# A planned transformer step on one Trainium2 core: ranges kept by column, a rotation's four swaps issued together, and the attention sink as one more column of the scores

## The chip, the cores and the metric

The kernel runs on one core of one Trainium2 chip. The metric is the device time of one execution in microseconds (us). A core has five engines that run side by side: TensorE (PE in the profile, its weight loads PEld), VectorE (DVE), ScalarE (ACT), GpSimd (POOL) and SyncE (SP), which here issues nearly all DMAs. Every engine works through its own list of instructions in order and waits on semaphores for the others.

## The reference

Two layers of a backbone work on 128 context tokens and 512 latent tokens at once (640 columns), with 2048 features. Each layer norms and modulates its input (adaLN), projects it, runs two mixers, gates the result and projects it out. The modulation is a product of a conditioning vector with a large matrix. The change lies in mixer A of layer 0, the windowed attention of eight query heads over two key/value heads, with rotated queries and keys and a sink logit per head:

```python
out = jnp.stack([a * cos - b * sin, a * sin + b * cos], axis=-2)      # rope_2d, for each axis
...
sk = jnp.broadcast_to(sink.astype(jnp.float32).reshape(1, 1, KV_A, g, 1, 1), s_ctx.shape[:-1] + (1,))
p = jax.nn.softmax(jnp.concatenate([s_band, s_ctx, sk], axis=-1), axis=-1)
pb = p[..., :3 * BAND_BLK]
pc = p[..., 3 * BAND_BLK:3 * BAND_BLK + L]
```

The sink takes part in the softmax's maximum and sum, and its own probability is dropped.

## The kernel before

**The work.** Activations lie feature-major: 128 features on the partitions, 640 tokens in the columns. A projection is cut into chunks of 128 output features. A chunk is 16 input tiles, times two halves of the columns, times three products of split float32 operands (`whi`/`wlo` with `acth`/`actl`, line 400): 96 matmuls of 320 or 322 columns. The chunks of the two layers are most of what TensorE does. In the later parts seven products stand for eight block products. While a chunk runs, the other engines split the next weights (ACT makes `whi`, POOL makes `wlo`), take the last chunk out of PSUM, and do the mixers' elementwise work. A slow background task makes the modulation: it loads a row block of the adaLN matrix, 256 KB (`adas<-ada`, `adas<-ada_g`), and reduces it on DVE (`CUSTOM_DVE_ANT_0 adas<-adas,bank`) or by POOL and ACT (`prod`).

**The order.** No scheduler of the compiler decides the order. The program is written out by `Trunk`, which keeps a clock of its own (`self.now`, TensorE's) and a cost model, `Pace`. `Pace.record` (reached from `Engine.call`, line 215, so nearly every VectorE, ScalarE and GpSimd row of the profile has that line) adds each instruction's reckoned time to its engine. `Pace.note` marks which columns of which tile are written and read until when, and `Pace.ready` says from when an operand can be used. The marks go by the ranges of `Pace.span`. Mixers are Python generators: `tick`, called every two matmuls of a chunk, resumes those whose reckoned waits are over (`until`, `bank`), and what they issue lands between the chunk's matmuls at that place. So a wrong reckoning costs no correctness, since semaphores guard all data, but it puts an instruction too early, and its engine then stands still with all that is queued behind it.

`Trunk.dma` (line 436) issues a DMA on SP at once if the model holds both ends ready within 0.1 us; otherwise it puts it into `pc.late`, and it is issued when it is reckoned ready or when another instruction touches its range.

**`span`.** `ap.offset` of an on-chip view counts in elements with the partition's stride in it. A view that starts at partition 32 of a tile 512 columns wide so gets a range that begins 32 rows further on, where no other view of that tile has marks.

**`rope`** (line 1606) rotates one head's 512 latent columns. Pairs of 32-partition strips of `q` are exchanged into `sw` by four DMAs of 64 KB, then DVE multiplies `q` by `cos`, POOL multiplies `sw` by `sin`, and DVE adds them. It is called ten times: for two keys and eight queries. `sw` is a strip of `arena` or of `Y`, so in the profile the swaps read `arena<-Y`, `Y<-arena` and `arena<-arena`. Three of the four swaps have a source that begins at partition 32 or more; the one that reads partition 0 has a range that the model has marked as being written.

**`even_head`** takes a head's five query blocks (one of context, four latent) through `blocks`: `s1` makes the scores and calls `soft1`, `soft2` scales, `s3` transposes the probabilities by TensorE (line 405, `bank<-ident,arena`) and ACT copies them out; one pass at the end multiplies with the values. `soft1` adds the mask and takes the row maximum (DVE), forms `nm` = -max(maximum, sink), and runs Exp with the row sum in `den` (ACT). Then ACT forms `es` = Exp(sink + nm). `soft2` adds `es` to `den` on ACT, takes the reciprocal on DVE and scales on ACT. Layer 1's attention calls the same two functions without a sink. `open_att` lays out the attention's part of SBUF; `pieces` are the four score buffers of 512 columns.

Of the kernel before, what the change touches and what calls it, by code (L numbers as in the profile page):

```python
# [13 lines left out]
AF = mybir.ActivationFunctionType  # L14
# [38 lines left out]
class Pace:  # L53
# [19 lines left out]
    def span(self, ap):  # L73

        if ap.space == bass.MemoryType.DRAM and ap.name not in (SPILL, YSP, SHIFTS, *KEEP):
            return None
        name = self.slot.get(ap.name, ap.name)
        if ap.space == PSUM:
            return name, 0, 1
        lo = hi = ap.offset  # L80
        for step, n in ap.ap[1:]:
            if step < 0:
                lo += step * (n - 1)
            else:
                hi += step * (n - 1)
        return name, lo, hi + 1
# [155 lines left out]
class Trunk:  # L242
# [1362 lines left out]
    def rope(self, q, sw):  # L1605
        nc = self.nc
        n = self.ropes = self.ropes + 1
        yield from self.wait(f"rope{n - 1}")
        s = slice(NCTX, T)
        for i, j in ((0, 1), (1, 0), (2, 3), (3, 2)):  # L1610
            self.dma(sw[32 * i : 32 * i + 32, :], q[32 * j : 32 * j + 32, s])
        yield from self.until(sw)
        nc.vector.tensor_tensor(q[:, s], q[:, s], self.cos, ALU.mult)
        nc.gpsimd.tensor_tensor(sw, sw, self.sin, ALU.mult)
        yield
        nc.vector.tensor_tensor(q[:, s], q[:, s], sw, ALU.add)
        self.flags.add(f"rope{n}")
        yield from self.until(q)
# [17 lines left out]
    def soft1(self, p, ps, mask, w, sinkcol):  # L1636

        nc = self.nc
        mx, nm, den = self.s("mx"), self.s("nm"), self.s("den")
        nc.vector.tensor_tensor_reduce(p[:, :w], ps[:, :w], mask, 1.0, NEG, ALU.add, ALU.max, mx)  # L1640
        if sinkcol is not None:
            nc.vector.tensor_scalar(nm, mx, sinkcol, -1.0, ALU.max, ALU.mult)
        else:
            nc.vector.tensor_scalar(nm, mx, -1.0, None, ALU.mult)
        self.act(p[:, :w], p[:, :w], AF.Exp, bias=nm, accum_out=den)
        es = None
        if sinkcol is not None:
            es = self.s("es")
            self.act(es, nm, AF.Exp, bias=sinkcol)
        return p[:, :w], den, es  # L1650

    def soft2(self, p, den, es):
        nc = self.nc
        if es is not None:
            nc.scalar.activation(den, es, AF.Identity, bias=den)
        nc.vector.reciprocal(den, den)
        if es is not None:
            nc.scalar.activation(p, p, AF.Copy, scale=den)
        else:
            nc.vector.tensor_scalar(p, p, den, None, ALU.mult)  # L1660
# [555 lines left out]
    def program(self):  # L2216
        nc, tc, d, Y = self.nc, self.tc, self.d, self.Y
# [95 lines left out]
        for h in range(4):  # L2313
# [18 lines left out]
            p = (f"gla_elem{h - 1}",) if h else ()  # L2332
# [22 lines left out]
        def open_att():  # L2355
            self.need("gla_done3")
            self.rp.__exit__(None, None, None)
            self.close_arena()
            self.arena(16.5)
            gx = self.t(self.ar_pool_, [128, 2 * T], "gx2")  # L2360
            L["hq"], L["gx"] = self.take(T, 3), Ring([gx[:, 0:T], gx[:, T : 2 * T]])
            L["hk"] = Ring([Y[:, 6, :], self.take()])
            L["av"] = self.take()
            L["vtoks"] = Ring([Y[:, 7, :], self.take()])
            L["sw"] = Ring([self.take(512), Y[:, 5, 0:512]])
            self.cos, self.sin, self.emask = (self.take(512) for _ in range(3))
            self.ckT, self.cv = (self.take(256).rearrange("p (a b) -> p a b", b=128) for _ in range(2))
            self.pieces = list(self.take(512, 4).list)
            self.pT = self.take(2048)

            def loads():
                for n, t in (("cos", self.cos), ("sin", self.sin), ("cache_attn_kT", self.ckT), ("emask", self.emask)):
                    self.dma(t, d[n])
                    yield 3.0
                    if n == "sin":
                        self.flags.add("rope0")
                self.dma(self.cv, d["cache_attn_v"])
                self.flags.add("att")
                yield

            self.spawn(loads(), first=True)

        gate_chunk(wE[28 + 15], self.yt(15), ("gla_done3",), "gt")
        do(open_att)
        def spill_y():
            self.room = self.rooms[2]
# [522 lines left out]
```

## Time and profile before

| what | us |
|---|---|
| median of three runs | 2083.95 |
| the three runs | 2080.47, 2083.95, 2084.21 |
| the profiled execution, its own time | 2084.38 |
| its span, first to last instruction | 2082.6 |
| TensorE busy in the span | 2040.6 (98%) |
| DVE, ACT, POOL busy | 1326.6, 1074.2, 1288.1 |
| mean granted TensorE clock | 0.996 |

The profiled execution's time is 1.8 us longer than its span, for what lies around the first and last instruction. By place in the span: the start with its own way of making the modulation takes about the first 185 us, mixer B (the gated linear attention) runs beside chunks from there to 485 us, mixer A from 485 to 830 us; then come the hand-over to the output projection of layer 0 (830 to 900 us) and the rest. A matmul's row counts from its start to the end of its drain, so rows of neighbours overlap: 0.31 us a row, one every 0.147 us.

### The profile page before, as it was taken

How to read it: one execution, taken by the hardware profiler on the slowest of the kernel's cores; microseconds unless marked ns; L12 is line 12 of the kernel's file. 1: busy time of each engine (PE TensorE's matmuls, PEld its weight loads, DVE VectorE, ACT ScalarE, POOL GpSimd, SP SyncE). 2: the span in 40 equal slices, each digit the busy share in tenths (PEclk: the TensorE clock that was granted, in tenths of full speed). 3: DMA queues.
4: the chain of work that ended last, by engine and by line, in shares of the span. 5: the costliest groups of instructions: out<-in, count | busy, mean ns of one | idle time of the engine just before them, and what ended most of it. 6: DMA issues, size and time to landing. Idle time of an engine off the chain costs nothing.

```text
span 2082.6 us, 40165 instructions
## 1 busy us (share of the span) xinstructions
PE 2040.6 (98%) x14329; PEld 1996.5 (96%) x14329; DVE 1326.6 (64%) x3040; ACT 1074.2 (52%) x2468; POOL 1288.1 (62%) x1081
## 2 busy tenths in 40 slices
PE   7999999999999999999999999999999999999997
PEld 6899999999899999999999999999999999999997
DVE  4657777676545665698586878887554554456444
ACT  5546555554665765444564434444444554454443
POOL 5655554456456554798855666656555577768884
PEclk9999999999999999999999999999999999999998
DMA  9966433446355454577634454444323344373427
GB/s 375 401 208 185 147 124 109 127 131 202 127 174 176 149 172 141 183 215 226 220 121 141 133 157 154 138 147 150 104 88 96 96 135 141 107 238 117 140 89 253
DMA packets 192697, 340.18 MB, mean 163 GB/s; under 512 B 20752, under 2 KB 70000, under 8 KB 192496
## 3 DMA queue, kind: packets, MB, share of 16 engines
q1 hardware_dynamic: 191296, 336.45, 49.8%
q8 instruction: 112, 1.84, 0.4%
q10 hardware_dynamic: 1200, 1.17, 0.2%
q14 instruction: 89, 0.73, 0.1%
HBM read 303.03 MB, written 31.88 MB: 161 GB/s over the span
## 4 chain that ended last, share of the span: by engine, by line
PE 81%; DMA 6%; DVE 6%; ACT 2%; issue 2%; POOL 1%; SPq 0%; DVEq 0%; ACTq 0%; POOLq 0%
PE bank L400 79%; PE bank L405 2%; DVE adas L215 2%; DVE arena L215 1%; DVE Y L215 1%; DMA raw<-crow_b 1%; ACT arena L215 1%; POOL wlo L215 1%; DMA Y<-xT 1%; DMA adas<-ada 1%; DMA adas<-gateT 1%; PE bank L1432 1%; SPq L436 0%; DVE bank L215 0%; DMA wraw<-w_even 0%
## 5 line engine op out<-in xcount | busy, mean ns | idle before, releaser
L400 PE MATMUL bank<-acth,whi 128*128 128x320 f32 (+3 forms) x3320 | 1019.9, 318 | 6.6 <-DVE YB L215 1.9
L400 PE MATMUL bank<-actl,whi 128*128 128x320 f32 (+3 forms) x3320 | 992.4, 310 | 0.0
L400 PE MATMUL bank<-acth,wlo 128*128 128x320 f32 (+3 forms) x3320 | 992.2, 310 | 0.1
L215 POOL TENSOR_TENSOR wlo<-wraw,whi 128x512 fp32r<-128x512 f32 (+1 forms) x446 | 569.1, 1288 | 418.1 <-ACT whi L215 353.3
L400 PEld LDWEIGHTS bank<-acth,whi 128*128 128x128 f32 (+1 forms) x3320 | 615.5, 188 | 14.1 <-issue 2.8
L400 PEld LDWEIGHTS bank<-actl,whi 128*128 128x128 f32 (+1 forms) x3320 | 616.2, 188 | 2.0
L400 PEld LDWEIGHTS bank<-acth,wlo 128*128 128x128 f32 (+1 forms) x3320 | 614.9, 188 | 0.5 <-POOL wlo L215 0.4
L215 POOL TENSOR_TENSOR wlo<-rs,whi 128x384 fp32r<-128x384 f32 x370 | 410.0, 1127 | 188.6 <-ACT whi L215 156.1
L215 ACT ACTIVATE whi<-wraw 128x512 fp32r<-128x512 f32 (+1 forms) x456 | 261.6, 589 | 126.2 <-PE bank L400 79.0
L215 ACT ACTIVATE whi<-rs 128x384 fp32r<-128x384 f32 x370 | 184.5, 519 | 75.5 <-PE bank L400 63.4
L400 PE MATMUL bank<-eh,whi 128*128 128x322 f32 (+1 forms) x666 | 208.7, 313 | 0.0
L400 PE MATMUL bank<-eh,wlo 128*128 128x322 f32 (+1 forms) x666 | 206.6, 310 | 0.5 <-POOL wlo L215 0.5
L400 PE MATMUL bank<-el,whi 128*128 128x322 f32 (+1 forms) x666 | 206.3, 310 | 0.0
L215 DVE CUSTOM_DVE_ANT_0 adas<-adas,bank,partg 128x256 bf16<-128x256 f32 (+1 forms) x293 | 158.5, 541 | 14.4 <-DMA adas<-ada_g 6.8
L215 DVE TENSOR_TENSOR wraw<-rs 128x768 f32<-128x768 f32 x74 | 100.7, 1361 | 99.4 <-DMA rs<-w_odd 51.9
L215 POOL TENSOR_TENSOR prod<-adas,mixrow 128x512 f32<-128x512 f32 x83 | 107.6, 1305 | 76.5 <-ACT prod L215 44.2
L215 ACT ACTIVATE arena<-arena,bc 128x512 f32<-128x512 f32 (+4 forms) x189 | 97.9, 540 | 71.2 <-DVE arena L215 66.3
L215 DVE TENSOR_TENSOR bank<-bank,sums 128x320 f32<-128x320 f32 (+1 forms) x148 | 70.9, 494 | 88.7 <-PE bank L400 66.5
L400 PEld LDWEIGHTS bank<-eh,wlo 128*128 128x128 f32 x666 | 125.1, 188 | 1.3 <-POOL wlo L215 1.3
L400 PEld LDWEIGHTS bank<-eh,whi 128*128 128x128 f32 x666 | 125.4, 188 | 0.1
L400 PEld LDWEIGHTS bank<-el,whi 128*128 128x128 f32 x666 | 125.4, 188 | 0.0
L215 DVE CUSTOM_DVE_ANT_0 adas<-adas,bank,part 128x512 bf16<-128x512 f32 x146 | 108.7, 744 | 15.9 <-DMA adas<-ada 13.0
(227 smaller groups left out, 2466.2 us busy)
## 6 DMA issues: line engine op xcount, KB each, us to landing
wraw<-w_even SPq DMA_DIRECT2D x176, 256.0 KB, 3.4
adas<-ada_g SPq DMA_DIRECT2D x128, 256.0 KB, 3.6
adas<-ada SPq DMA_DIRECT2D x128, 256.0 KB, 3.7
rs<-w_odd SPq DMA_DIRECT2D x50, 384.0 KB, 3.3
wraw<-w_odd SPq DMA_DIRECT2D x74, 256.0 KB, 3.7
wraw<-w_out SPq DMA_DIRECT2D x60, 256.0 KB, 3.5
rs<-w_odd SPq DMA_DIRECT2D x50, 256.0 KB, 4.0
Y<-ada SPq DMA_DIRECT2D x24, 512.0 KB, 7.5
```

What stands on the lines that cost most here:

```text
L215: return f(*args, **kw)
L400: self.nc.tensor.matmul(out, lhsT, rhs, start=start, stop=stop, **kw)
L405: self.nc.tensor.transpose(out, in_, self.ident[:k, :k])
L1432: nc.tensor.matmul(o, c, w, start=j < 4, stop=j >= 12)
```

## The change

`span` takes the partition's part off the offset of an on-chip view, so that ranges are columns of a tile, whatever the partition. `rope` waits, before its first swap, until the model holds both `sw` and the latent columns of `q` ready, and then issues the four swaps one after another. In `soft1`, DVE copies the head's sink into the column behind the scores, and the Exp runs over one column more, so that `den` holds the whole sum; `es` and its addition to `den` go. Score buffers are 516 columns wide, and the arena is 32 columns larger. All that stands after the first line is one line further down in the changed kernel (the helpers' lines are 216, 401, 406 and 437).

```diff
@@ Pace.span
-        lo = hi = ap.offset
+        lo = ap.offset if ap.space == bass.MemoryType.DRAM else ap.offset % ap.ap[0][0]
+        hi = lo
@@ Trunk.rope
         s = slice(NCTX, T)
+        pc = self.pace
+        while (w := pc.ready("q", [pc.span(sw)], [pc.span(q[:, s])]) - self.now) > 0.05:
+            yield w
         for i, j in ((0, 1), (1, 0), (2, 3), (3, 2)):
             self.dma(sw[32 * i : 32 * i + 32, :], q[32 * j : 32 * j + 32, s])
@@ Trunk.soft1
-        self.act(p[:, :w], p[:, :w], AF.Exp, bias=nm, accum_out=den)
-        es = None
         if sinkcol is not None:
-            es = self.s("es")
-            self.act(es, nm, AF.Exp, bias=sinkcol)
-        return p[:, :w], den, es
+            nc.vector.tensor_copy(p[:, w : w + 1], sinkcol)
+        n = w + (sinkcol is not None)
+        self.act(p[:, :n], p[:, :n], AF.Exp, bias=nm, accum_out=den)
+        return p[:, :w], den, n > w
@@ Trunk.soft2
-        if es is not None:
-            nc.scalar.activation(den, es, AF.Identity, bias=den)
         nc.vector.reciprocal(den, den)
-        if es is not None:
+        if sink:
             nc.scalar.activation(p, p, AF.Copy, scale=den)
@@ open_att
-            self.arena(16.5)
+            self.arena(16.55)
-            self.pieces = list(self.take(512, 4).list)
+            self.pieces = list(self.take(516, 4).list)
```

What that does to the order of instructions, at three places. First SyncE, where the second rotation (of the first query head) issues its swaps, `Y<-arena`; `adas` and `wraw` are loads of the adaLN matrix and of weights. Before:

```order
L436 DMA wraw<-w_even 128x512
L436 DMA adas<-ada 128x512 x2
L436 DMA Y<-arena_4751 32x512 x3
L436 DMA adas<-ada 128x512
L436 DMA Y<-arena_4751 32x512
```

In the change:

```order
L437 DMA wraw<-w_even 128x512
L437 DMA adas<-ada 128x512 x3
L437 DMA Y<-arena_4748 32x512 x4
L437 DMA wraw<-w_even 128x512
L437 DMA adas<-ada 128x512
```

The load that stood between the third and the fourth swap now stands ahead of the four. In the order before, six of the ten rotations have such a load in that place; in the change none has.

Second TensorE, where the scores of that head's first latent block stand (`bank_70`, the first that read rotated columns), among a chunk's matmuls. Before, from the 2921st row after the program's first on:

```order
L400 MATMUL bank_67<-actl,whi 128x320
L400 MATMUL bank_67<-acth,wlo 128x320
L400 MATMUL bank_70<-arena_4751 128x128
L400 MATMUL bank_70<-Y,arena_4751 128x256
L400 MATMUL bank_69<-acth,whi 128x322
```

In the change, from the 2933rd row on:

```order
L401 MATMUL bank_69<-actl,whi 128x322
L401 MATMUL bank_69<-acth,wlo 128x322
L401 MATMUL bank_70<-arena_4748 128x128
L401 MATMUL bank_70<-Y,arena_4748 128x256
L401 MATMUL bank_67<-acth,whi 128x320
```

These scores stand 12 chunk matmuls later; the transposes of the values, a good 150 rows earlier, have the same row in both.

Third ScalarE, at that head's first softmaxes (`den` the sums, `prod` and `whi` other work). Before:

```order
L531 ACT_TABLE_LOAD
L215 ACTIVATE arena_4751,den_5288<-arena_4751,nm_5287 128x128
L215 ACTIVATE es_5293<-nm_5287,small 128x1
L215 ACTIVATE den_5288<-es_5293,den_5288 128x1
L215 ACTIVATE arena_4751<-arena_4751,den_5288 128x128
L215 ACTIVATE arena_4751,den_5318<-arena_4751,nm_5317 128x384
```

In the change:

```order
L532 ACT_TABLE_LOAD
L216 ACTIVATE arena_4748,den_5308<-arena_4748,nm_5307 128x129
L216 ACTIVATE prod_107,psum<-prod_107 128x512
L216 ACTIVATE whi<-wraw 128x512
L216 ACTIVATE arena_4748<-arena_4748,den_5308 128x128
L216 ACTIVATE arena_4748,den_5339<-arena_4748,nm_5338 128x385
```

Two instructions of one column are gone per softmax, and the Exp has one column more. Over the program TensorE has as many rows as before, and ScalarE has 26 table loads in both. The order on all engines is unchanged up to mixer B (row 1185 on TensorE). In mixers A and B the mixers' instructions stand some rows earlier or later among the chunks. Behind mixer A's last matmul TensorE's order is the same again but for buffer numbers; on the other engines that holds from the place in the output projection of layer 0 on where the background task ends.

More of the change, by code (lines that the diff above doesn't have):

```diff
@@ L1644, in soft1, with soft2 @@
             nc.vector.tensor_scalar(nm, mx, -1.0, None, ALU.mult)
-        self.act(p[:, :w], p[:, :w], AF.Exp, bias=nm, accum_out=den)
-        es = None
         if sinkcol is not None:
-            es = self.s("es")
-            self.act(es, nm, AF.Exp, bias=sinkcol)
-        return p[:, :w], den, es
-    def soft2(self, p, den, es):
+            nc.vector.tensor_copy(p[:, w : w + 1], sinkcol)
+        n = w + (sinkcol is not None)
+        self.act(p[:, :n], p[:, :n], AF.Exp, bias=nm, accum_out=den)
+        return p[:, :w], den, n > w
+    def soft2(self, p, den, sink):
         nc = self.nc
-        if es is not None:
-            nc.scalar.activation(den, es, AF.Identity, bias=den)
         nc.vector.reciprocal(den, den)
-        if es is not None:
+        if sink:
             nc.scalar.activation(p, p, AF.Copy, scale=den)
```

## Prediction

> **What bounds the kernel now.** I read the page's busy times first, then the windows by stage, then what TensorE waited for, then the chain of waits where it did. The page:
>
> ```profile
> span 2082.6 us, 40165 instructions
> PE 2040.6 (98%) x14329; PEld 1996.5 (96%) x14329; DVE 1326.6 (64%) x3040; ACT 1074.2 (52%) x2468; POOL 1288.1 (62%) x1081
> ```
>
> TensorE is busy all but 42 us of the span, so a change that leaves its matmuls alone can win only idle time, or time at a lower clock. Where that is, the windows by stage show (length, then busy time and count by engine, then granted clock, DMA share, GB/s):
>
> ```profile
> 0.00:185.00 185.00, 170.39 (x1685) 156.50 (x1686) 108.47 (x242) 97.27 (x217) 111.48 (x100) 0.99 0.88 314
> 185.00:485.00 300.00, 297.13 (x2044) 291.33 (x2043) 220.57 (x390) 166.70 (x338) 149.35 (x104) 1.00 0.40 126
> 485.00:830.00 345.00, 335.94 (x2219) 322.50 (x2219) 198.88 (x569) 212.73 (x554) 182.03 (x139) 1.00 0.52 165
> 830.00:900.00 70.00, 67.45 (x454) 66.28 (x453) 51.17 (x96) 34.24 (x73) 53.89 (x40) 1.00 0.57 176
> 900.00:2050.00 1150.00, 1149.80 (x7800) 1141.50 (x7799) 729.28 (x1712) 552.71 (x1270) 777.46 (x686) 1.00 0.46 145
> 2050.00:2083.00 33.00, 19.91 (x138) 18.36 (x136) 18.25 (x37) 10.59 (x19) 13.85 (x15) 0.83 0.71 256
> ```
>
> The start (14.6 us idle) and the end (13.1) keep their order of instructions, and from 900 to 2050 us there is 0.2 us to be had. What the change can reach is mixer A from 485 to 830 us: 345.00 - 335.94 = 9.06 us idle. TensorE's waits in that window (total, times, longest):
>
> ```profile
> PE bank L400 <- DVE arena L215: 4.8, 2, 3.3
> PE bank L405 <- ACT arena L215: 4.3, 7, 1.1
> ```
>
> The first row is scores that wait for rotated columns, the second transposes that wait for scaled probabilities. The chain of waits in that window tells what stands behind them (start, length):
>
> ```profile
> 574.38 4.30 DMA Y<-arena
> 578.75 0.69 DVE arena L215
> 579.45 0.09 DVE den L215
> 579.55 0.63 ACT arena L215
> 580.23 0.55 PE bank L405 x3
> ...
> 763.21 3.22 DMA arena<-arena
> ...
> 774.18 0.33 PE bank L405
> ```
>
> A fourth swap lands late, DVE stands at the rotation's product in front of another head's reciprocal, ACT then scales late, and TensorE's transposes wait. So both rows above are largely one cause: the rotation's product is placed by the landing of the first swap, the only one that the model sees.
>
> **The swaps.** The worst place is the first query head's rotation: SP's issues, POOL's and DVE's products, TensorE's scores, from the timelines, and under them the DMA view of 526 to 537 us (median time to landing):
>
> ```profile
> 527.22 1.78 SPq L436 DMA_DIRECT2D Y<-arena  x3
> 529.11 0.53 SPq L436 DMA_DIRECT2D adas<-ada  x1
> 529.68 0.51 SPq L436 DMA_DIRECT2D Y<-arena  x1
> ```
>
> ```profile
> 534.44 1.26 POOL L215 TENSOR_TENSOR Y<-Y,arena 128x512 f32<-128x512 f32 x1 [4.04 <-DMA Y<-arena]
> ```
>
> ```profile
> 537.98 0.49 PE L400 MATMUL bank<-arena 128*128 128x128 f32 x2 [3.35 <-DVE arena L215]
> ```
>
> ```profile
> adas<-ada SPq DMA_DIRECT2D x3, 256.0 KB, 4.7
> Y<-arena SPq DMA_DIRECT2D x4, 64.0 KB, 2.0
> ```
>
> The fourth swap is issued 0.57 us behind a 256 KB load and lands at about 534.4, 4.7 us after its issue, where the median is 2.0. Issued right behind the third it would start at 527.22 + 3 x 0.59 = 529.0 and land at about 531.0, 3.4 us earlier. The order puts these scores 12 chunk matmuls later, 12 x 1149.80 / 7800 = 1.8 us. Together 5.2 us against a wait of 3.35: it goes. If the load that is now ahead of the four delays them as much as it does now, 3.35 - 1.8 = 1.6 us of it stays. What is late next there is the DVE queue: each adaLN reduction that the order puts ahead of the product adds to it, which is in these ends.
>
> That wait costs a second time, by the clock (seventh number) right after it:
>
> ```profile
> 538.00:540.00 2.00, 2.00 (x10) 1.93 (x10) 1.55 (x7) 0.94 (x4) 2.00 (x2) 0.73 0.38 131
> 540.00:542.00 2.00, 1.67 (x7) 1.28 (x6) 1.61 (x6) 1.46 (x6) 0.29 (x1) 0.50 0.71 192
> 542.00:544.00 2.00, 2.00 (x15) 2.00 (x14) 1.23 (x5) 1.78 (x7) 1.29 (x1) 0.92 0.21 71
> 676.00:678.00 2.00, 2.00 (x14) 1.95 (x15) 1.93 (x8) 1.06 (x4) 2.00 (x2) 1.00 0.72 221
> ```
>
> 2 x (0.27 + 0.50 + 0.08) = 1.7 us are lost to it; the stage's other wait for DVE (4.8 - 3.3 = 1.5 us, just before 676) left the clock alone. I take the 1.7 as won, since a rest of 1.6 us at most is nearer to that one. [...]
>
> How much of the 9.06 us goes: the same planner, without swaps, leaves 300.00 - 297.13 = 2.87 us idle in mixer B (185 to 485 us). At that rate mixer A would keep 345 / 300 x 2.87 = 3.3 us, so 5.8 go. The bounds are 0 and 9.06.
>
> **The sink.** What ACT and DVE do on one column now, in 485 to 830 us (busy, mean ns, idle before), and a copy of another size:
>
> ```profile
> L215 ACT ACTIVATE den<-es,den 128x1 f32<-128x1 f32 x40 | 11.6, 290 | 0.1
> L215 ACT ACTIVATE es<-nm,small 128x1 f32<-128x1 f32 x40 | 11.2, 280 | 0.0
> L215 DVE TENSOR_SCALAR nm<-mx,small 128x1 f32<-128x1 f32 x40 | 8.6, 214 | 1.4
> L215 DVE RECIPROCAL den<-den 128x1 f32<-128x1 f32 x40 | 6.5, 164 | 43.5 <-ACT den L215 43.4
> L215 DVE COPY arena<-bank 128x128 f32<-128x128 f32 x8 | 2.3, 290 | 10.4 <-PE bank L405 10.4
> ```
>
> ACT loses 40 x (0.290 + 0.280) = 22.8 us, and each softmax's chain 0.57 us. DVE gains 40 copies of one column; the trace has none. At most they cost like the copy of 128 columns (0.29, 11.6 us in all), at least nothing, since an added instruction can't shorten an in-order engine's list; I take 0.164, the nearest in shape, from SBUF to SBUF like it: 6.6 us. DVE is idle for 345 - 199 = 146 us of this stage, 43.4 of them at the reciprocal waiting for `den`, which the removed ACT steps shorten, so the copies lie beside idle time; ahead of each Exp they put 0.16 us where 0.57 goes behind it. None of this is TensorE's, and the planner puts the next step earlier accordingly: 0 us on the path. If the cover went, the 6.6 us would be DVE's, spread over 40 softmaxes.
>
> [...]
>
> **The rest.** The order has 10 more changes between chunk matmuls and short ones in mixer A. Their price, from a chunk matmul behind a short one and its neighbour:
>
> ```profile
> 511.17 0.39 PE L400 MATMUL bank<-acth,whi 128*128 128x320 f32 x1
> 511.39 0.30 PE L400 MATMUL bank<-actl,whi 128*128 128x320 f32 x1
> ```
>
> 10 x 0.09 = 0.9 us slower (0 to 0.9). The wider score buffers move nothing in time, and the `span` line in mixer B moves pieces by some matmuls at a place with 2.87 us idle: 0, with 2 us either way.
>
> **Sum.** Against the profiled execution's own 2084.38 us: -5.8 - 1.7 + 0.9 = -6.6, 2077.8. The median of the runs is 0.4 us below that execution; on it the forecast is 2077.5.
>
> **Rivals.** (1) The waits come back elsewhere: loads still stand right ahead of the four swaps at most of the ten rotations, and behind a queue of loads all four can be late, as between 594 and 602.5 us:
>
> ```profile
> arena<-arena SPq DMA_DIRECT2D x4, 64.0 KB, 5.8
> ```
>
> 3.8 us later than the median of 2.0. Against it: at that place no TensorE wait followed. It decides where the scores come soonest, at the first head: if 3.35 + 1.7 stay there, the sum is -(5.8 - 3.35) + 0.9 = -1.6, 2082.4 on the median. Chance 0.28.
>
> [...] Chance 0.05. (3) Slower by a new long wait: each like the worst one costs 3.35 + 1.7 = 5.05 us; three of them in the replanned stages (185 to 900 us) give 2084 + 8.6 = 2092.5. The order's places are better reckoned than before, which speaks against three. Chance 0.06. That the change doesn't do what it says is ruled out by the order: four swaps in one row.
>
> **Numbers.** The forecast's case has 0.61; its own ends are 2083.95 - 9.06 - 1.7 = 2073.2 and, with half of the 6.6 won, 2080.6. The range takes in rival 1 and a measurement's spread: 2073 to 2084.5, which leaves out the slower cases and little else. A measurement of this kernel can tell about 0.2%, 4.2 us, from no change (its runs spread over 3.7). Faster by more (below 2079.8) 0.60, within 0.28, slower 0.12.
>
> **What would show it.** Right: in 485 to 830 us TensorE's idle time is 2 to 5 us, the row of scores waiting for DVE is gone or below 1.7, the granted clock stays 1.00; four swaps in one SP row, landing 2 to 4 us after issue; no `es` rows, DVE's wait for `den` well below 43; 40 copies of 0.1 to 0.3 us. Wrong: 8 us or more idle there, a stretch at clock 0.5 in 185 to 900 us, or copies with a mean above 0.4 us.

## The result, and the profile after

The changed kernel takes 2072.57 us (median of six runs, 2071.37 to 2073.77) beside 2083.78 for the kernel before in the same rounds (2080.47 to 2084.30): ratio 0.995, interval 0.9939 to 0.996, so 8.3 to 12.7 us less. Measured again later, it was 2074.54 beside 2083.38, ratio 0.9952 (0.994 to 0.9964). The forecast was 2077.5, 6.4 us less: the right side, and 3 to 5 us too little.

The page's busy times, after:

```profile
span 2069.7 us, 40165 instructions
PE 2035.8 (98%) x14329; PEld 1995.2 (96%) x14329; DVE 1312.3 (63%) x3058; ACT 1060.2 (51%) x2411; POOL 1298.7 (63%) x1092
```

TensorE was idle 42 us of the span before and is idle 33.9 now. Mixer A now runs from 472 to 818 us. Its window, and three at the hand-over behind it (length, busy time and count by engine, granted clock, DMA share, GB/s):

```profile
472.00:818.00 346.00, 345.13 (x2303) 333.76 (x2302) 225.21 (x670) 208.42 (x513) 197.24 (x152) 1.00 0.58 182
830.00:832.00 2.00, 1.22 (x7) 1.10 (x8) 2.00 (x6) 1.76 (x4) 2.00 (x3) 0.99 0.01 4
832.00:834.00 2.00, 2.00 (x9) 2.00 (x8) 2.00 (x6) 2.00 (x6) 2.00 (x2) 0.50 0.41 130
834.00:836.00 2.00, 2.00 (x11) 2.00 (x11) 2.00 (x3) 1.11 (x2) 2.00 (x2) 0.65 0.00 1
```

346.00 - 345.13 = 0.87 us idle, where before had 9.06 in a stage of the same length. In this execution the granted clock falls to 0.50 at the hand-over, where the trace of before shows 1.00. TensorE's waits from 472 to 900 us:

```profile
PE bank L401 <- ACT eh L216: 1.7, 1, 1.7
PE bank L406 <- ACT arena L216: 0.8, 2, 0.6
PE bank L401 <- POOL wlo L216: 0.3, 1, 0.3
PE bank L401 <- DVE sums L216: 0.2, 1, 0.2
```

The scores' wait for DVE is gone, and the transposes' wait for ACT is 0.8 us in 2 places, where it was 4.3 in 7. SyncE at the first query head's rotation:

```profile
521.94 2.40 SPq L437 DMA_DIRECT2D adas<-ada  x3
524.39 2.42 SPq L437 DMA_DIRECT2D Y<-arena  x4
526.91 0.53 SPq L437 DMA_DIRECT2D wraw<-w_even  x1
```

The four swaps stand in one row with the load ahead of them. And the softmax's instructions of one column, with the Exp behind them, in 472 to 818 us (busy, mean ns, idle before):

```profile
L216 DVE TENSOR_SCALAR nm<-mx,small 128x1 f32<-128x1 f32 x40 | 8.6, 214 | 1.4
L216 DVE RECIPROCAL den<-den 128x1 f32<-128x1 f32 x40 | 6.3, 159 | 3.4 <-ACT arena L216 3.3
L216 DVE COPY arena<-small 128x1 f32<-128x1 f32 x40 | 5.8, 144 | 0.0
L216 ACT ACTIVATE arena<-arena,nm 128x385 f32<-128x385 f32 x16 | 9.9, 619 | 8.9 <-DVE arena L216 8.9
```

The Exp of the kernel before with 384 columns, in 485 to 830 us:

```profile
L215 ACT ACTIVATE arena<-arena,nm 128x384 f32<-128x384 f32 x16 | 9.9, 619 | 3.8 <-DVE nm L215 3.7
```

The copies take 0.144 us each, the Exp no more than with 384 columns (619 ns in both), and the reciprocal, which stood idle 43.5 us before, now 3.4.

**Where the time went, by stage.** Both kernels run the same sequence of chunk matmuls (those that read split weights: `whi`, `wlo`, and near the start `suhi` and `sulo`), so the time from the start of one to the start of a later one can be set side by side. In us, worked out from the start times in each trace, with the first, 961st, 2401st, 4321st, 5301st and last but one chunk matmul as the limits, and all kernels told of below in one table. TensorE's long wait at the hand-over still falls into mixer A's column, a lower clock behind it into the next.

| kernel (traced execution) | start | mixer B | mixer A | hand-over and next | up to the last chunk |
|---|---|---|---|---|---|
| before, first | 187.1 | 278.7 | 364.8 | 145.7 | 1078.7 |
| before, second (e11) | 189.7 | 278.6 | 359.7 | 145.6 | 1079.5 |
| changed, first | 187.9 | 276.6 | 353.3 | 146.8 | 1077.6 |
| changed, second (e5) | 189.7 | 276.7 | 354.5 | 146.8 | 1077.9 |
| ranges alone (e1) | 189.5 | 276.6 | 353.8 | 146.6 | 1079.5 |
| rotation's wait alone (e2) | 188.9 | 278.6 | 353.6 | 146.4 | 1079.1 |
| ranges and wait (e3) | 190.2 | 276.6 | 354.5 | 148.7 | 1079.3 |
| sink alone (e4) | 188.1 | 278.6 | 355.5 | 146.1 | 1077.7 |
| sink alone, again (e12) | 188.0 | 278.6 | 358.0 | 146.9 | 1077.6 |
| four more copies in the chain (e6) | 188.8 | 276.6 | 359.1 | 145.3 | 1077.9 |
| the same ahead of it (e9) | 189.9 | 276.6 | 354.6 | 145.3 | 1078.0 |
| load between swaps (e7) | 189.0 | 276.7 | 357.8 | 146.8 | 1077.9 |
| load ahead of swaps (e8) | 190.2 | 276.6 | 355.7 | 145.3 | 1077.7 |
| the copy ahead of the chain (e10) | 188.0 | 276.6 | 356.8 | 148.5 | 1078.1 |

The start differs by up to 3 us from execution to execution. Mixer B has 2.0 us less in every kernel that has the new ranges, to 0.1 us the same each time. The last column has 1.4 us less on average in the kernels that have the sink's part, and 0.6 at the least. Mixer A carries most, and differs by 5.1 us between two executions of the same kernel before. In e3 and e8 it also holds a halving of the clock near 513 us: granted 0.63 and 0.51 in the two windows from 512 to 516 us of e3, 0.95, 0.50 and 0.69 in the three from 512 to 518 us of e8, worth 2 x 0.86 = 1.7 us by the windows of either, or 1.5 as at the hand-over (146.8 - 145.3 in the next column; the last section shows one of e8's windows).

### The profile page after: what moved, and what is told of

The parts are those of the page before. It is cut to its first block, busy times and chain, and to the rows that moved or that the text cites. A ratio compares the mean times of both kernels' runs of the same rounds, so it can differ in the third digit from the quotient of the medians.

```text
span 2069.7 us, 40165 instructions
## 1 busy us (share of the span) xinstructions
PE 2035.8 (98%) x14329; PEld 1995.2 (96%) x14329; DVE 1312.3 (63%) x3058; ACT 1060.2 (51%) x2411; POOL 1298.7 (63%) x1092
## 4 chain that ended last, share of the span: by engine, by line
PE 86%; DMA 6%; DVE 4%; issue 2%; ACT 1%; POOL 1%; SPq 0%; DVEq 0%; ACTq 0%; POOLq 0%
PE bank L401 83%; PE bank L406 2%; DVE adas L216 1%; DMA adas<-ada 1%; POOL wlo L216 1%; DMA raw<-crow_b 1%; DVE arena L216 1%; DVE Y L216 1%; DMA Y<-xT 1%; PE bank L1433 1%; DMA more<-ada 0%; DMA wraw<-w_even 0%; DMA adas<-gateT 0%; DMA adas<-ada_g 0%; DMA adas<-shift_s 0%
## 5 line engine op out<-in xcount | busy, mean ns | idle before, releaser
L216 POOL TENSOR_TENSOR prod<-adas,mixrow 128x512 f32<-128x512 f32 x94 | 121.3, 1299 | 77.4 <-ACT prod L216 49.0
L216 DVE CUSTOM_DVE_ANT_0 adas<-adas,bank,part 128x512 bf16<-128x512 f32 x136 | 101.2, 744 | 14.1 <-DMA adas<-ada 11.2
```

Source lines behind the costliest of these rows:

```text
L216: return f(*args, **kw)
```

## The experiments

**Theory and rivals.** My theory was the forecast's: the gain is the rotation's, since the planner now knows when all swaps have landed, and they land together. Rivals: only the ranges count (theory M), or only the standing together (Q), or it is the sink's shorter way (S). The first four kernels take the change apart; they ran with the same 33 runs of before (median 2082.39).

**e1: the ranges alone.** The new `span` line in the kernel before, nothing else.

```diff
-        lo = hi = ap.offset
+        lo = ap.offset if ap.space == bass.MemoryType.DRAM else ap.offset % ap.ap[0][0]
+        hi = lo
```

> Only the line of the ranges is changed; the rotation doesn't wait for its operands and the sink stays on ScalarE as before. In the order five of ten rotations still have a load between the third and the fourth swap, but the model now sees all four landings. Theory M (the gain comes from true marks: the rotation's product and the scores are placed by the last landing): nearly all of the 11.2 us between the two kernels, 8 to 12 us below the kernel before, 2072 to 2076, and TensorE's idle time in mixer A 2 to 4 us. Theory Q (the gain comes from swaps that stand together on SyncE): at most 3 us below the kernel before, 2081 to 2084, with the scores' wait for DVE back at 2 us or more. Theory S (the gain comes from the sink's way): no more than 5 us below the kernel before.

Measured: 2076.60 (2072.89 to 2081.28, 11 runs), ratio 0.9976 (0.9968 to 0.9985), so 5.0 us less (3.1 to 6.7). That lies between what M and Q expected, and at S's bound of 5. The trace shows both halves: 2.0 us from mixer B, which has no rotation, and mixer A at 353.8. TensorE's wait for DVE, which Q expected back with 2 us or more, is 0.2 us in 475 to 828 us, though a load stands between the third and the fourth swap at the first query head here too.

**e2: the rotation's wait alone.**

```diff
+        pc = self.pace
+        while (w := pc.ready("q", [pc.span(sw)], [pc.span(q[:, s])]) - self.now) > 0.05:
+            yield w
         for i, j in ((0, 1), (1, 0), (2, 3), (3, 2)):
```

> Only the rotation's wait for its operands is added: all four swaps stand together, but ranges are as before, so the model sees the landing of one swap alone; the sink stays on ScalarE. Theory Q (swaps together): 6 to 12 us below the kernel before, 2072 to 2078. Theory M (true marks): the product is still placed too early behind a queue of loads, so waits of 2 us or more stay and the time is 0 to 4 us below the kernel before, 2080 to 2084. Theory S (sink): no more than 5 us below.

Measured: 2078.99 (2075.72 to 2082.52, 11 runs), ratio 0.9984 (0.9975 to 0.9993), 3.3 us less (1.5 to 5.2). In time that is M's range (0 to 4) and not Q's (6 to 12), but the waits of 2 us or more that M expected are not there. The traced execution was the shortest of the eleven, with this for waits in 475 to 828 us:

```profile
PE bank L405 <- ACT arena L215: 1.8, 2, 0.9
PE bank L400 <- DVE arena L215: 0.3, 1, 0.3
```

So neither theory holds alone: swaps that stand together take the scores' wait away even where the model sees one landing of four, and true marks do so even where a load stands between the swaps.

**e3: both, the sink as before.**

> Both changes to the rotation (ranges and wait), the sink on ScalarE as before. My theory (the rotation): 8 to 11 us below the kernel before, 2073 to 2076; mixer A's idle time 1 to 3 us. The rival (the sink: ScalarE's 22.8 us and DVE's 43 us of waiting for the sums held the transposes up): only the first head's wait and its clock go, 3.4 + 1.7 = about 5 us below, 2078 to 2080, and transposes still wait for ScalarE by some 4 us.

Measured: 2076.64 (2073.89 to 2081.24, 11 runs), ratio 0.9972 (0.9962 to 0.9982), 5.8 us less (3.7 to 7.9). The two parts hardly add: together they give little more than the ranges alone, as far as intervals of about 2 us to either side can tell. The edit is the change's first two pieces. It falls short of my 8 to 11, and is nearer to the rival's 5. Mixer A's idle time, 353.00 - 350.92 = 2.08 us in 475 to 828 us, is inside my 1 to 3. The traced execution is 1.8 us above the median; its clock was at 0.51 from 514 to 516 us, and its 148.7 us in the table's fourth column hold 2.4 us of waits for split weights.

**e4: the sink alone**, with the wider score buffers, in the kernel before.

> Only the sink as a column (with the wider score buffers); ranges and swaps as before. My theory (the rotation): 0 to 2 us below the kernel before, 2082 to 2084; the scores' wait of about 3 us at the first query head stays, and the clock drops behind it; DVE's wait for the sums goes all the same, from 43 to under 5 us, without a gain. The rival (the sink): 4 to 6 us below, 2078 to 2080.

Measured: 2079.86 (2074.91 to 2082.57, 11 runs), ratio 0.9984 (0.9975 to 0.9993), 3.3 us less (1.5 to 5.2). My theory gave 0 to 2, which the interval still touches. What decides is the changed kernel, ratio 0.995 (0.9939 to 0.996), beside e3's 0.9972 (0.9962 to 0.9982): the sink's part is worth something on TensorE's path. The two shares, 5.8 and 3.3, add to 9.1 of the 10.0 to 10.4 that the ratios of the whole change give, so the parts are worth nearly as much apart as together. TensorE's waits in 475 to 828 us:

```profile
PE bank L405 <- ACT arena L215: 1.8, 4, 0.8
PE bank L400 <- DVE arena L215: 0.9, 1, 0.9
```

DVE's idle time ahead of the reciprocal is 0.7 us here, where it was 43.5. The scores' wait, which I expected to stay at 3 us, is 0.9, though the order at that place has the load between the swaps as before. That made the trace of before itself doubtful; e11 takes it up.

**e5: the changed kernel again**, the measure for e6 to e8 (16 runs of before, median 2083.38).

> The changed kernel once more, as the measure for the three kernels beside it. 8 to 12 us below the kernel before, in the same rounds. If the parts measured alone simply add up (the rotation 5.8 us, the sink 3.3 us), 9 us; if they need each other, 11 or more. [...]

Measured: 2074.54 (2072.24 to 2075.20, 5 runs), ratio 0.9952, 10.0 us less (7.5 to 12.5), which leaves both the 9 and the 11 open. The hand-over's wait came again, with 2.32 us beside 1.70 in the first trace, and the granted clock was low again behind it: 0.79, 0.50 and 0.86 in the three windows from 834 to 840 us.

**e6: five copies in the chain.** The sink's copy is issued four more times where it stands, between the row maximum and the Exp.

```diff
             nc.vector.tensor_copy(p[:, w : w + 1], sinkcol)
+            for _ in range(4):
+                self.tc.nc.vector.tensor_copy(p[:, w : w + 1], sinkcol)
```

> The changed kernel with each of the 40 sink copies issued five times, unknown to the planner: 160 copies of 0.144 us more, 23 us more for DVE, and 0.58 us more ahead of each Exp. Theory C (the sink's gain of 3.3 us comes from the softmax's chain being 0.4 us shorter, so that transposes are no longer late): it is given back, 3 to 6 us above the changed kernel, with TensorE's transposes waiting for ScalarE by 3 us or more in mixer A. Theory D (DVE's idle time covers the copies, and the sink's gain lies elsewhere): 0 to 1.5 us above. If DVE were the bound of the stage, it would be up to 23 us above.

Measured: 2079.63 (2077.34 to 2082.88, 10 runs), 5.1 us above e5, ratio to before 0.998 (0.9971 to 0.9989). Theory C holds: more than the sink's 3.3 us is given back, and not the 23 us that DVE has more. The copies' row in mixer A, and TensorE's waits:

```profile
L1652 DVE COPY arena<-small 128x1 f32<-128x1 f32 x160 | 24.6, 154 | 5.5
```

```profile
PE bank L406 <- ACT arena L216: 3.2, 10, 0.9
```

Ten transposes wait for scaled probabilities, none for more than 0.9 us: not one stall, but many small ones. e6 lengthens chain and DVE's work at once, so it can't tell these two apart.

**e9: the same four copies ahead of the chain**, before the mask's addition, where DVE stands waiting for the scores (2.7 + 14.1 + 13.5 = 30.3 us ahead of e5's 40 additions; e9 to e12 ran with 9 runs of before, median 2084.57).

```diff
+        if sinkcol is not None:
+            for _ in range(4):
+                self.tc.nc.vector.tensor_copy(p[:, w : w + 1], sinkcol)
         nc.vector.tensor_tensor_reduce(p[:, :w], ps[:, :w], mask, 1.0, NEG, ALU.add, ALU.max, mx)
```

> The changed kernel with the four extra copies of each softmax, unknown to the planner, ahead of the mask's addition, where DVE often stands waiting for the scores, instead of between the maximum and the Exp. DVE has the same 23 us more as with five copies in the chain, which cost 5.1 us. Theory C (the length of a softmax's chain counts): most of the extra copies lie in DVE's wait for the scores, 0 to 2 us above the changed kernel, so 2073 to 2076.5. Theory O (DVE's occupation counts): 4 to 6 us above, 2078 to 2081.

Measured: 2073.59 (2070.71 to 2075.57, 5 runs), ratio 0.9948 (0.9935 to 0.9962), as the changed kernel. The same work costs nothing there:

```profile
L1646 DVE COPY arena<-small 128x1 f32<-128x1 f32 x160 | 23.9, 149 | 4.1
```

```profile
PE bank L406 <- ACT arena L216: 0.9, 1, 0.9
PE bank L401 <- DVE arena L1646: 0.4, 1, 0.4
```

TensorE's order is the same in e5, e6 and e9. From the start of `nm` to the start of the scaling, the 40 softmaxes take 119.3 us together in e5, 118.1 in e9 and 144.7 in e6 (worked out from the start times in each trace). e6 and e9 have the same copies; only e6 has the chain longer, by 25.4 us, and only e6 is slower. So it is the length of the chain from maximum to scaled probabilities that TensorE pays for, not DVE's occupation. e6 gives the price of a lengthening that the planner doesn't know of: 5.1 / 25.4 = 0.20 us for each.

The sink's part takes 0.57 us from each chain and puts 0.144 in: 40 x 0.426 = 17.0 us. As run, the stretch fell by more, from 154.1 us (e11) to 122.1 (e4). Times 0.20 that is 3.4 or 6.4 us; e4 measured 3.3. But the planner knows of this shortening and moves the later steps with it, and e12 below finds only a part of the gain in mixer A. So the price shows that the chain can matter, not that it makes up the 3.3. Whether ACT's own 22.8 us count beside that was not tried.

**e7 and e8: a load of 128 KB between the third and the fourth swap, or ahead of the four**, in the changed kernel. The planner doesn't know of it, and nothing reads it. The arena is wider in both, for the strip that the load fills.

```diff
+            if i == 3:
+                self.nc.sync.dma_start(self.spare, self.d["ada_1"][n % 4, :, 0:256])
             self.dma(sw[32 * i : 32 * i + 32, :], q[32 * j : 32 * j + 32, s])
```

> The changed kernel with a load of 128 KB into a spare strip between the third and the fourth swap of each rotation, unknown to the planner; nothing reads it. Theory L (a late last swap makes the scores and transposes late): the fourth swap lands 1 to 2.5 us later than in the changed kernel, waits of 0.5 to 2 us come back at some rotations, 1 to 4 us above the changed kernel. If a rotation's slack covers it: within 1 us of the changed kernel.

> The same load of 128 KB ahead of the four swaps, which stay together. Theory L (it is the last landing that counts, however the swaps stand): the last swap lands as late as with the load between, so 1 to 4 us above the changed kernel, as there. Theory Q (it counts that the four stand together): within 1 us of the changed kernel, while the load between costs more.

Measured, beside e5's 2074.54: between, 2077.24 (2073.52 to 2077.95, 5 runs), ratio to before 0.9963 (0.9951 to 0.9976); ahead (`i == 0` in the diff), 2074.29 (2071.26 to 2078.32, 6 runs), ratio 0.9953 (0.9939 to 0.9967). SyncE at the first query head of the one, TensorE's rows behind it, and SyncE of the other:

```profile
527.98 1.79 SPq L437 DMA_DIRECT2D Y<-arena  x3
529.82 0.58 SPq L1616 DMA_DIRECT2D arena<-ada  x1
530.44 0.51 SPq L437 DMA_DIRECT2D Y<-arena  x1
```

```profile
537.87 0.49 PE L401 MATMUL bank<-arena 128*128 128x128 f32 x2 [1.04 <-DVE arena L216]
540.96 0.33 PE L406 MATMUL bank<-ident,arena 128*128 128x128 f32 x1 [1.27 <-ACT arena L216]
```

```profile
528.48 0.42 SPq L1616 DMA_DIRECT2D arena<-ada  x1
529.00 2.42 SPq L437 DMA_DIRECT2D Y<-arena  x4
```

With the load between, the fourth swap lands 3.6 us after its own issue and 6.1 after the first's; with it ahead, the last lands 4.2 us after the first's issue, as in e5. Only the load between brings the first head's waits back. (e8's traced execution has its clock at 0.50 from 514 to 516 us, ahead of this place.) Theory L is right that a late last landing costs TensorE time, and wrong that both loads make it equally late; so Q's outcome holds for this pair. The two intervals overlap, so that the 2.7 us between e7 and e5 rest on the place of the waits more than on the times.

**e11: the kernel before once more**, for its trace.

> The kernel before once more, for its trace. By the forecast's reading the fourth swap at the first query head stands behind the load in every execution and lands over 4 us after its issue, and the scores wait over 2.5 us for it, with the clock halved behind. If that landing is chance: a wait of 1 us or less there, as in the kernel with the sink's part alone, whose order of swaps is the same at that place and whose fourth swap landed after 3.2 us; mixer A's idle time then is 4 to 7 us, not 9, and the execution is below 2082.

One execution, 2082.85 us. The fourth swap's row of the DMA view, issued 0.57 us behind the load as in the first trace, and TensorE's rows behind it:

```profile
Y<-arena SPq DMA_DIRECT2D x1, 64.0 KB, 3.2
```

```profile
538.61 0.49 PE L400 MATMUL bank<-arena 128*128 128x128 f32 x2 [1.37 <-DVE arena L215]
...
541.36 0.33 PE L405 MATMUL bank<-ident,arena 128*128 128x128 f32 x1 [0.94 <-ACT arena L215]
```

```profile
538.00:540.00 2.00, 1.39 (x9) 1.34 (x10) 1.96 (x7) 0.34 (x2) 2.00 (x3) 1.00 0.32 111
540.00:542.00 2.00, 1.06 (x8) 0.80 (x8) 1.35 (x8) 1.43 (x6) 0.93 (x1) 1.00 0.49 145
```

It lands after 3.2 us, not over 4, the scores wait 1.37 and not 3.35, and the clock stays at 1.00. For chance I had given a wait of 1 us or less and a time below 2082; both came out somewhat above, but nearer to that than to the over 2.5 us and the halved clock of the other reading. The long wait and the clock's loss of the first trace were that execution's. Mixer A still took 359.7 us, and its idle time was 345.00 - 339.25 = 5.75 from this row, inside the 4 to 7 that I gave for chance:

```profile
484.00:829.00 345.00, 339.25 (x2254) 326.26 (x2253) 203.61 (x580) 215.19 (x559) 185.26 (x141) 1.00 0.52 167
```

**e12: the sink alone once more.**

> The kernel with the sink's part alone once more, for its trace: its first traced execution was the shortest of its eleven. Idle time of mixer A 4 to 6 us. If the landing at the first query head is chance: a wait of the scores anywhere from 0 to 3.5 us, and the time 2075 to 2083 by that and by the clock behind it.

One execution, 2078.61. The scores waited 1.3 us, mixer A took 358.0, and its idle time in 475 to 828 us was 353.00 - 349.51 = 3.49 us, under the 4 to 6 that I expected. Against e11 that is 1.7 us less in mixer A and 1.9 less in the last column, together 3.6: the 3.3 of e4 again. (e4's own trace has 4.2 and 1.8.) The second part lies where no softmax has a sink, so the chain can't be its cause.

**e10: the one copy ahead of the chain**, known to the planner; the version that e6 and e9 point to.

```diff
+        if sinkcol is not None:
+            nc.vector.tensor_copy(p[:, w : w + 1], sinkcol)
         nc.vector.tensor_tensor_reduce(p[:, :w], ps[:, :w], mask, 1.0, NEG, ALU.add, ALU.max, mx)
...
-        if sinkcol is not None:
-            nc.vector.tensor_copy(p[:, w : w + 1], sinkcol)
```

> The changed kernel with its one copy of the sink ahead of the mask's addition; the planner knows of it. If the chain's length counts as five copies priced it, 5.1 us for 40 times 0.58 us, then 40 times 0.144 us less are worth 1.3 us: 0.5 to 2 us below the changed kernel, about 2073. If the planner's own slack decides, since it puts the next step as much earlier: no change within 1 us.

Measured: 2077.21 (2073.62 to 2079.15, 5 runs), ratio to before 0.9966 (0.9953 to 0.9978): 2.7 us above e5, and 3.6 above e9, which ran in the same rounds. The intervals overlap with both. Both expectations missed. TensorE's waits in 475 to 910 us:

```profile
PE bank L406 <- ACT arena L216: 2.9, 4, 1.3
PE bank L401 <- ACT eh L216: 1.6, 1, 1.6
PE bank L401 <- POOL wlo L216: 1.1, 2, 0.6
PE bank L401 <- ACT bc L216: 1.0, 1, 1.0
PE bank L401 <- ACT whi L216: 1.0, 1, 1.0
```

The planner, told of a shorter chain, put the transposes elsewhere among the chunks, and this order has waits that the changed kernel's has not: 1.0 and 1.3 us near 675 us, and three for split weights at the hand-over. As run, the stretch from `nm` to the scaling is longer in this order, not shorter: 134.8 us for the 40 softmaxes beside 119.3 in e5. Why the order draws these waits was not followed further. What the planner doesn't know of (e9) it could not spend.

## Why the prediction was right or wrong

**Right: where the time is.** TensorE's idle time in mixer A was the largest thing to be had, and it fell from 9.06 us (5.75 in e11) to 0.87 (353.00 - 351.38 = 1.62 in e5). The four swaps stand together, the `es` rows are gone, the wait for `den` fell to 3.4 us, the scores' wait went, and e7 brings that wait back by a load between the swaps alone. That both rows of waits "are largely one cause" holds in part: the transposes' 4.3 us fell to 2.1 by the rotation alone (e3), and to 1.8 and 2.2 by the sink alone (e4, e12).

**Failed: "None of this is TensorE's, and the planner puts the next step earlier accordingly: 0 us on the path".** This is the largest error. The sink's part measured 3.3 us (1.5 to 5.2). I looked at DVE's idle time, which does cover the copies (e9), and took cover for the work as cover for the chain. But chain time can reach the transposes: what the planner doesn't know of costs 0.20 us for each microsecond (e6). How much of the 3.3 us comes that way is not shown, since about 1.4 of it lies behind the hand-over, in the table's last column.

**Mis-sized: what stays idle.** "At that rate mixer A would keep 3.3 us" was an analogy with mixer B; 0.9 to 1.6 stayed, below the 2 to 5 that I had named as the sign of being right.

**Right by luck: the clock's 1.7 us.** They were lost in the execution that I read and won in the changed one, but the second trace of before has no such loss (e11). Both traces of the changed kernel lose as much at the hand-over: the table's fourth column has 146.8 us with the halved clock, and 145.3 in e6, e8 and e9, whose order there is the same and whose clock stays at 1.00. As a property of the kernels, the term is nothing, or against the change. And the fourth swap's 4.7 us to landing (4.6 by the DMA view), on which "3.4 us earlier" rests, was 3.2 in e11. The 5.8 us of idle time have the same luck in them: between the second executions, e11 and e5, 5.75 - 1.62 = 4.1 us went. One profiled execution showed a wait of the right cause with a size of its own. (From 2083.95 a gain of 6.6 leads to 2077.4, not 2077.5; nothing hangs on it.)

**Not there: "10 x 0.09 = 0.9 us slower".** From e11 to e5 the intervals into and out of runs of short matmuls rise in number from 144 to 154, but their sum, from start to start without waits, falls from 14.18 to 13.83 us, worked out from the trace. All 2338 intervals between matmuls of mixer A, without their waits, sum to 352.2 us in e11 and 350.5 in e5. The price was read from one side only: behind the row of 0.39 the next chunk matmul starts after 0.23 us instead of 0.147, but the row itself starts 0.03 us behind the short one ahead of it.

**Outside the sum: mixer B and the rest.** The `span` line was put at "0, with 2 us either way" in mixer B; it gave 2.0 there, the same in each of the kernels that have it. The 1.4 us in the last column, in kernels with the sink's part, were not forecast. TensorE's order there is the same; from the 5301st to the 9101st chunk matmul e5 gains 0.9 us on e11, and all but two of these 3800 intervals differ by 15 ns or less. The difference goes with the kernel and not with the execution: over the whole column, 98% of e12's intervals are within 1 ns of e5's, and 99% of e11's within 1 ns of the first trace of before, but only 61% of e11's within 1 ns of e5's. The cause stays open.

**The sum anew**, e11 to e5: mixer B -1.9, mixer A -5.2, hand-over +1.2, rest -1.6, makes -7.5, of the 7.65 us between these two executions.

**The rivals.** (1) Waits that come back elsewhere: not in mixer A, but at the hand-over in part, where e10 has three waits that the changed kernel has not. (2) The slower case with the chance of 0.05, by slow copies, for which a mean above 0.4 us was the sign: no. 200 copies in e6 have means of 144 and 154 ns, while POOL is busy for 200.66 / 353.00 = 0.57 of 475 to 828 us, where before had 0.53 of mixer A. (3) New long waits: the longest in 185 to 900 us of the first trace is the hand-over's 1.70, which was there before with 1.93.

**A sign that misled.** I had named a stretch at clock 0.5 in 185 to 900 us as a sign of being wrong. There is one, 832 to 834 us with 0.50, in a kernel that is 11 us faster.

## What to carry to other kernels

Cover for an engine's work is not cover for a chain (the same copies cost 5.1 us in e6's chain and nothing ahead of it in e9): ask of each instruction that a chain gains or loses how soon the bound engine needs the chain's end, and test it by putting the same work into the chain and beside it. Where a planner places work by landings, what it must know is the last landing; issue pieces that are needed together without a load among them (the last landed 6.1 us after the first's issue in e7, 4.2 in e8). And where a single wait carries a forecast, read it in a second execution first: here two traces of one kernel had 3.35 and 1.37 us at the same instruction.

## What was unexpected of the hardware

In these traces the granted clock did not go by the length of the idle time alone. At the hand-over TensorE has one long wait, with chunk matmuls on both sides. The wait's row in the changed kernel, whose windows with clock 0.50 and 0.65 are shown above, and that of e12 with its windows:

```profile
830.78 0.72 PE L401 MATMUL bank<-acth,whi 128*128 128x320 f32 x2 [1.70 <-ACT eh L216]
```

```profile
837.77 0.72 PE L400 MATMUL bank<-acth,whi 128*128 128x320 f32 x2 [2.54 <-ACT eh L215]
```

```profile
838.00:840.00 2.00, 2.00 (x14) 1.93 (x14) 2.00 (x7) 2.00 (x6) 2.00 (x2) 1.00 0.24 67
840.00:842.00 2.00, 2.00 (x15) 2.00 (x14) 2.00 (x2) 2.00 (x5) 2.00 (x3) 1.00 0.17 65
```

Behind an idle time of 1.70 us the clock was at 0.50, behind one of 2.54 it stayed at 1.00. Of the other traces, 2.32 (e5, 0.50) and 2.12 (e7, 0.54) had a window of 2 us at a low clock behind them; behind 1.93 (before), 1.76 (e11), 1.75 (e9), 1.66 (e8) and 2.20 (e6) it stayed at 1.00. Near 512 us even two waits under 1 us, with one transpose of 0.33 us between them, had 0.50 behind them in e8 (rows, and a window behind them):

```profile
511.39 0.33 PE L406 MATMUL bank<-ident,arena 128*128 128x128 f32 x1 [0.80 <-ACT arena L216]
512.58 0.66 PE L406 MATMUL bank<-ident,arena 128*128 128x128 f32 x4 [0.85 <-ACT arena L216]
```

```profile
514.00:516.00 2.00, 2.00 (x9) 2.00 (x9) 1.93 (x6) 1.52 (x5) 1.75 (x2) 0.50 0.68 176
```

In e5, waits of 0.77 and 0.85 us at the same two rows left it at 1.00. So my "a rest of 1.6 us at most is nearer to that one" rested on the one wait of 1.5 us that left the clock alone, and drew a line that these traces do not have; what decides instead is not shown. Where TensorE's order at the hand-over is the changed kernel's, the table's fourth column has 146.8 us with the low clock (both traces of the changed kernel, and e7) and 145.3 without it (e6, e8 and e9): such a halving cost 1.5 us.
